# A diffusion layer on one core: gated tiles through another DMA queue, two early operand loads, and background steps placed later

## The chip, the cores and the metric

The kernel runs on one core of a Trainium2 chip. The core has five engines that each work through their own list of instructions in order: TensorE (PE, matrix products; PEld is its weight load), VectorE (DVE), ScalarE (ACT), GpSimd (POOL) and SyncE (SP, which here only issues DMAs). They wait for each other by semaphores. DMAs are carried by 16 shared DMA engines; an engine that issues one puts it in a queue, and here nearly all are issued by SP.

The metric is the device time of one execution in microseconds (us), lower being better.

## What is computed

One layer over 1024 latent tokens and 256 context tokens, 1024 channels wide, all in float32: a half-step SwiGLU feed-forward, then token mixing (a Fourier part and a bidirectional chunked mLSTM, merged by gates), then a second half-step feed-forward on the latent tokens.

```python
def swiglu(u, w13, w2):
    a, b = jnp.split(u @ w13, 2, axis=-1)
    return (jax.nn.silu(a) * b) @ w2

def half_ffn(h, shift, scale, gate, g_pre, g_post, w13, w2):
    u = modulate(rmsnorm(h, g_pre), shift, scale)
    return h + 0.5 * gate * rmsnorm(swiglu(u, w13, w2), g_post)

def ada_params(cvec, w, b):
    m = jax.nn.silu(cvec) @ w + b
    return m.reshape(cvec.shape[0], N_ADA, 1, D_MODEL)

def reference(...):
    ml = ada_params(c, w_ada[l], b_ada[l])
    mc = ada_params(c_ctx[None], w_ada[l], b_ada[l])
    h_lat = half_ffn(h_lat, ml[:, 0], ml[:, 1], ml[:, 2], g[0], g[1], w13_a[l], w2_a[l])
    h_ctx = half_ffn(h_ctx, mc[:, 0], mc[:, 1], mc[:, 2], g[0], g[1], w13_a[l], w2_a[l])
    h_lat, h_ctx_new = token_mixing(...)
    h_lat = half_ffn(h_lat, ml[:, 6], ml[:, 7], ml[:, 8], g[4], g[5], w13_b[l], w2_b[l])
    return h_lat
```

The hidden width of a feed-forward is 2816, the nine modulation vectors of each stream (shift, scale and gate for three sub-layers, called chunks 0 to 8 below) come from `ada_params`.

## The kernel before

**Products.** Every float32 operand is split by `split_act` into a rounded high part (ACT, L145) and the rest (DVE, L146); weights go the same way (L140/L141 in `wunit`, or `split_act`). A product of 128x128 by 128x512 is three matmuls, all at L153 in `mm3`. The large products of the two feed-forwards use a two-by-two scheme with seven products in place of eight, so DVE also adds and subtracts blocks of weights and of operands (L727 and others).

**The feed-forward.** `ffn_in` computes the first product pair by pair of column tiles, 11 pairs. Its operands for the second block of tokens are made in the background by `operands`, whose sums of two tiles run on GpSimd (L455, L456). Gated tiles ("m" and "t", 128x512) are the blocks that the seven products of the second matrix need; `gated` (L475) or the sums at L582/L583 finish a tile, and `put` (L478/L479) stores it to the DRAM scratch `gx`: four "m" tiles and three "t" tiles for each pair, 77 for each `ffn_in`, so 154 in all. L614 reads some of them back. `wino_out` is the second product: for n in (1, 6, 7, 4, 5, 3, 2) and each k it calls `operand` (L772 to L777), which loads a tile of `gx` into a "t" slot (L774) and splits it into two "g" slots, takes the weights (L733, L738), and issues 12 matmuls. The first `ffn_in` ends and the first `wino_out` begins at about 483 us of the trace, the second pair of stages meets at about 2510 us.

**Slots.** Tiles come from tags with a fixed number of slots ("t" 8, "m" 5, "g" 36, "ld" 2, "u" 16, "wa" 2, "b" and others); a new tile waits until the last user of its slot has finished.

**Background work.** Generators are advanced a step (a `yield`) at a time by `tick`. `later(gen, rate=r)` puts a generator in the list with a rate, and `tick(part)` adds part x rate to a credit that pays for steps. `wino_out` ticks 1/8 for each group of three matmuls, so at a rate of 3.5 one step falls on about 2.3 groups. Behind the first `wino_out` run `load_x` for the context (transposes at L375) and `ada_rest` for chunks 2 and 3, then the context's `prenorm` and `ada_rest` for chunk 4. `ada_rest` computes half a chunk for two streams: eight loads of weights (L247), 16 multiply-adds on DVE (L251, L253), one split for each stream (L145, L146), the sum over the partitions as matmuls on PE (L263), a copy of the row (L266), and transposes of the row back into columns (`ada_cols`, L275, added up at L279). There is one step between a split and its row sums, and one between the copy and the transposes. During the mLSTM heads `ada_rest` for one stream and chunks 5 to 8 runs as `self.side`, at a rate of 3.0. Behind the second `wino_out` runs `to_tokens` at a rate of 1.0, once for each block of 512 tokens: for each of eight channel tiles a load of `h` (L1556), a step, four transposes into a "qc" bank of PSUM (L1560), a copy (L1562) and a store to `h2t` (L1563).

**Order.** The code order is the order of calls above; the instructions of one engine are put in a final order by a scheduler when the program is built, and each engine then keeps that order. An instruction that waits holds up all that follow it on its engine. SP carries loads of weights, loads of `gx`, stores and background loads in one such list.

Of the kernel before, what the change touches and what calls it, by code (L numbers as in the profile page):

```python
# [15 lines left out]
P = 128  # L16
D = 1024
ND = D // P
SEQ = 1024
CTX = 256  # L20
# [14 lines left out]
class Kernel:  # L35
# [200 lines left out]
            nc.scalar.copy(row[:2, :], pt[:2, :])  # L236
            self.ada_cols(row, (0, 1), ch, 0)

    def ada_rest(self, streams, chunks, tags=("wa", "u", "u", "b"), halves=(0, 1)):
        nc = self.nc  # L240
        w = self.a["w_ada"][0]
        for ch in chunks:
            for hf in halves:
                acc = {s: self.s512(tags[1]) for s in streams}
                for k in range(ND):
                    t = self.s512(tags[0])
                    nc.sync.dma_start(t, w[k * P : (k + 1) * P, ch * D + hf * TB : ch * D + (hf + 1) * TB])  # L247
                    yield
                    for s in streams:
                        if k == 0:  # L250
                            nc.vector.tensor_scalar_mul(acc[s], t, self.sc[:, k, s : s + 1])  # L251
                        else:
                            nc.vector.scalar_tensor_tensor(acc[s], t, self.sc[:, k, s : s + 1], acc[s],  # L253
                                                           op0=ALU.mult, op1=ALU.add)
                yield
                for s in streams:
                    ah, al = self.s512(tags[2], F32R), self.s512(tags[2], F32R)
                    self.split_act(ah, al, acc[s])
                    if s == streams[0]:
                        pr = self.aux()  # L260
                    yield
                    for i, part in enumerate((ah, al)):
                        nc.tensor.matmul(pr[:2, :], self.sel[:, s, :], part, start=s == streams[0] and i == 0,  # L263
                                         stop=s == streams[-1] and i == 1)
                row = self.s512(tags[3])
                nc.scalar.copy(row[:2, :], pr[:2, :])  # L266
                yield
                self.ada_cols(row, streams, ch, hf)

    def ada_cols(self, row, streams, ch, hf):  # L270
# [205 lines left out]
        return gate  # L476

    def put(self, p, t, gx, n):  # L478
        self.nc.sync.dma_start(gx[n - 1, p * P : (p + 1) * P, :], t)  # L479

    def pair_weights(self, w, q, n0, W, p1s):

# [236 lines left out]
    def wino_out(self, w2, gx, tokens, done):  # L719
# [50 lines left out]
            return [(hi[:, c], lo[:, c]) for c in cs]  # L770

        def operand(n, k):  # L772
            t = self.s512("t")
            nc.sync.dma_start(t, gx[n - 1, k * P : (k + 1) * P, :])  # L774
            hi, lo = self.s512("g", F32R), self.s512("g", F32R)
            self.split_act(hi, lo, t)
# [774 lines left out]
    def to_tokens(self, scr, b, dst):  # L1551

        nc = self.nc
        for d in range(ND):
            t = self.s512("u")
            nc.sync.dma_start(t, scr[d * P : (d + 1) * P, b * TB : (b + 1) * TB])  # L1556
            yield
            pt = self.aux("qc")
            for j in range(4):
                nc.tensor.transpose(pt[:, j * P : (j + 1) * P], t[:, j * P : (j + 1) * P], self.ident)  # L1560
            o = self.s512("u")
            nc.scalar.copy(o, pt)  # L1562
            nc.sync.dma_start(dst[b * TB : (b + 1) * TB, d * P : (d + 1) * P].rearrange("(j p) c -> p j c", p=P),  # L1563
                                o.rearrange("p (j c) -> p j c", j=4))

    def final(self, h2t):
# [35 lines left out]
    def run(self):  # L1602
# [29 lines left out]
        for p in range(3):  # L1632
# [5 lines left out]
        gx = self.scratch([7, FF // 2, TB], "gx")  # L1638
        rc1, r1 = [], [[], []]
        self.ffn_in(w13, 11, u, U, gx, 6, mid)  # L1640
        self.later(self.load_x(a["ctx"][0], CTX, "c", xc, tag="u"), self.ada_rest([0, 1], [2, 3], "uuuu"),
                   rate=3.5)
        self.credit = -9.0
        uc = ctx_u([self.slot("u", F32R) for _ in range(ND)])

        def ctx_in():
            yield from self.prenorm(self.reload(xc[0], CTX), xc[1:], CTX, 1, 0, uc)
            yield from self.ada_rest([0, 1], [4])
        self.later(ctx_in(), rate=3.5)
        res = [[None] * ND for _ in range(NB)]  # L1650

# [52 lines left out]
        self.side_rate = 3.0  # L1704
        for h in range(HEADS):
            if h == 1:
                self.side = self.ada_rest([0], [5, 6, 7, 8], ("ld", "acc", "rb", "b"))
            if h % 2 == 0:
                v = [[self.slot("u") for _ in range(4)] for _ in range(2)]
                br = self.bias_row(C_V + h * DH)  # L1710
# [99 lines left out]
```

## Time and profile before

| | |
|---|---|
| median of 3 runs | 2758.67 us (2755.25 to 2763.62) |
| the profiled execution | 2761.97 us |
| its span in the trace | 2760.1 us |
| PE busy | 2661.3 us, 96% |
| DVE busy | 1857.2 us, 67% |
| ACT busy | 1106.8 us, 40% |
| POOL busy | 100.6 us, 4% |
| DMA traffic | 472.51 MB, mean 171 GB/s |
| mean granted PE clock | 0.986 |

The share of an engine is that of its busy time in the span. An average over the span hides that stages have different limits, so the prediction reads single stretches: views of the busy time in stretches of 60 us, the waits of an engine by the instruction that ended them, and timelines, where each row has a start in us, a duration, the engine and line, the tiles out<-in, the number of instructions in the row, and in brackets the idle time before it and what ended that. A granted clock under 1.00 means that PE ran its matmuls more slowly.

### The profile page before, as it was taken

What the parts mean: (1) busy time and instruction counts of PE and PEld (TensorE: products, weight loads), DVE (VectorE), ACT (ScalarE), POOL (GpSimd) and SP (SyncE); (2) the same over time, 40 slices, a digit from 0 to 9 for tenths busy, and PEclk for the clock granted to TensorE, in tenths of its full rate; (3) what the DMA queues carried; (4) which work ended last, traced back from release to release, by engine and by line L of the source; (5) the groups of instructions that cost most, each with busy time, mean ns of one, the idle gap of its engine ahead of it and who ended that gap; (6) DMA issues with size and microseconds to landing.
All of it is one profiled execution on the core that took longest, in us unless ns stands there. A gap on an engine that the chain in (4) does not pass through costs nothing.

```text
span 2760.1 us, 33923 instructions
## 1 busy us (share of the span) xinstructions
PE 2661.3 (96%) x11657; PEld 2114.7 (77%) x11657; DVE 1857.2 (67%) x3341; ACT 1106.8 (40%) x1893; POOL 100.6 (4%) x217
## 2 busy tenths in 40 slices
PE   8899999998999999999999999999999999998998
PEld 5688888776877777777777778778887788887776
DVE  5688887899786438565363674555667887863765
ACT  4543332444454337233333333433345433333552
POOL 1100000000000001000000000000001000000000
PEclk9999999999999999999999999999999999999999
DMA  9765454857686545325223452356556654536874
GB/s 300 242 206 164 155 167 133 309 190 252 210 252 211 170 134 173 102 69 155 79 77 103 133 142 77 94 150 196 181 157 210 183 169 153 168 107 198 293 247 139
DMA packets 426012, 472.51 MB, mean 171 GB/s; under 512 B 25497, under 2 KB 264642, under 8 KB 425840
## 3 DMA queue, kind: packets, MB, share of 16 engines
q1 hardware_dynamic: 424448, 468.53, 54.2%
q0 software_dynamic: 1248, 1.75, 0.2%
q8 instruction: 92, 1.51, 0.2%
q14 instruction: 80, 0.66, 0.1%
q10 hardware_dynamic: 144, 0.07, 0.0%
HBM read 373.21 MB, written 97.04 MB: 170 GB/s over the span
## 4 chain that ended last, share of the span: by engine, by line
PE 75%; DVE 9%; DMA 8%; issue 4%; ACT 2%; SPq 1%; POOL 0%; DVEq 0%; POOLq 0%; ACTq 0%
PE mm L153 67%; DMA m<-r_l 2%; PE aux L1147 2%; PE qc L1332 1%; DVE u L253 1%; DVE wl L141 1%; DVE g L146 1%; DMA ld<-in_w_ada_dram 1%; DMA ld<-h 1%; DMA u<-h 1%; DMA ld<-hn 1%; PE mm L234 1%; DMA t<-gx 0%; ACT wh L140 0%; DVE wl L146 0%
## 5 line engine op out<-in xcount | busy, mean ns | idle before, releaser
L153 PE MATMUL mm<-g,wh 128*128 128x512 f32 (+1 forms) x2552 | 839.6, 409 | 11.9 <-ACT g L145 5.0
L153 PEld LDWEIGHTS mm<-g,wh 128*128 128x128 f32 (+1 forms) x2552 | 484.2, 192 | 122.2 <-ACT wh L145 6.0
L153 PE MATMUL mm<-g,wl 128*128 128x512 f32 (+1 forms) x1276 | 510.7, 402 | 3.4 <-DVE wl L146 3.3
L153 PE MATMUL mm<-g,o 128*128 128x512 f32 x2112 | 497.7, 394 | 0.0
L153 PEld LDWEIGHTS mm<-g,o 128*128 128x128 f32 x2112 | 396.9, 188 | 93.7
L141 DVE TENSOR_TENSOR wl<-wr,wh 128x1024 fp32r<-128x1024 f32 x226 | 278.8, 1234 | 223.9 <-ACT wh L140 223.2
L140 ACT CAST wh<-wr 128x1024 fp32r<-128x1024 f32 x226 | 236.3, 1046 | 352.5 <-PE mm L153 307.3
L153 PE MATMUL mm<-wh,g 128*128 128x512 f32 x1032 | 331.2, 399 | 6.6 <-ACT g L145 3.9
L153 PEld LDWEIGHTS mm<-g,wl 128*128 128x128 f32 (+1 forms) x1276 | 243.8, 191 | 59.0 <-DVE wl L146 5.6
L153 PE MATMUL mm<-u,wh 128*128 128x512 f32 (+1 forms) x848 | 268.4, 398 | 7.5 <-DVE m L704 4.9
L153 PEld LDWEIGHTS mm<-wh,g 128*128 128x128 f32 x1032 | 194.1, 188 | 54.5 <-ACT g L145 4.1
L153 PE MATMUL mm<-wl,g 128*128 128x512 f32 x516 | 205.1, 397 | 0.0
L153 PEld LDWEIGHTS mm<-u,wh 128*128 128x128 f32 (+1 forms) x848 | 159.8, 190 | 46.0 <-DVE m L704 5.4
L153 PE MATMUL mm<-wh,u 128*128 128x512 f32 x544 | 176.4, 399 | 0.0
L153 PE MATMUL mm<-u,wl 128*128 128x512 f32 (+1 forms) x424 | 167.3, 397 | 2.3 <-DVE wl L141 2.3
L582 DVE TENSOR_TENSOR t<-mm,t 128x512 f32<-128x512 f32 x128 | 88.1, 688 | 78.8 <-PE mm L153 78.6
L146 DVE TENSOR_TENSOR g<-t,g 128x512 fp32r<-128x512 f32 x154 | 103.0, 687 | 38.9 <-ACT g L145 32.1
L153 PEld LDWEIGHTS mm<-wh,u 128*128 128x128 f32 x544 | 102.0, 188 | 22.5
L145 ACT CAST o<-wa 128x512 fp32r<-128x512 f32 x88 | 54.6, 622 | 156.0 <-PE mm L153 144.8
L145 ACT CAST wh<-wr 128x1024 fp32r<-128x1024 f32 (+1 forms) x72 | 62.5, 870 | 131.9 <-PE mm L153 55.2
L153 PEld LDWEIGHTS mm<-wl,g 128*128 128x128 f32 x516 | 97.2, 188 | 23.0 <-issue 0.7
L153 PE MATMUL mm<-wl,u 128*128 128x512 f32 x272 | 108.8, 400 | 2.1 <-DVE wl L141 2.1
(469 smaller groups left out, 3432.8 us busy)
## 6 DMA issues: line engine op xcount, KB each, us to landing
wr<-in_w_a_dram SPq DMA_DIRECT2D x124, 512.0 KB, 4.4
t<-gx SPq DMA_DIRECT2D x174, 256.0 KB, 4.0
wr<-in_w_in_dram SPq DMA_DIRECT2D x80, 512.0 KB, 3.8
wr<-in_w_b_dram SPq DMA_DIRECT2D x70, 512.0 KB, 4.5
gx<-m SPq DMA_DIRECT2D x88, 256.0 KB, 4.2
gx<-t SPq DMA_DIRECT2D x66, 256.0 KB, 4.3
ld<-in_w_ada_dram SPq DMA_DIRECT2D x64, 256.0 KB, 2.8
ld<-h SPq DMA_DIRECT2D x48, 256.0 KB, 3.8
```

What stands on the lines that cost most here:

```text
L140: nc.scalar.copy(hv, rv)
L141: nc.vector.tensor_tensor(lv, rv, hv.bitcast(F32), op=ALU.subtract)
L145: self.nc.scalar.copy(hi, src)
L146: self.nc.vector.tensor_tensor(lo, src, hi.bitcast(F32), op=ALU.subtract)
L153: mul = lambda x, y, start, stop: self.nc.tensor.matmul(out, x, y, start=start, stop=stop, skip_group_check=grown)
L234: nc.tensor.matmul(pt[:2, :], self.sc[:, k, :], t, start=k == 0, stop=k == ND - 1)
L253: nc.vector.scalar_tensor_tensor(acc[s], t, self.sc[:, k, s : s + 1], acc[s], op0=ALU.mult, op1=ALU.add)
L582: add = lambda o, x, y: nc.vector.tensor_tensor(o, x, y, op=ALU.add)
L1147: nc.tensor.matmul(pt[:, :257], kw[:, i * P : (i + 1) * P], vaug, start=True, stop=True)
L1332: nc.tensor.matmul(pt[:, :257], at(q, i, c), C[:, i * 257 : (i + 1) * 257], start=i == 0, stop=i == 1)
```

## The change

Four edits. `put` issues its store on GpSimd's queue in place of SP's. `operand` takes the first two tiles of n = 1 from "ld" in place of "t". `ada_rest` has a parameter `lag`, the number of further steps between a split and its row sums, and between the copy of the row and its transposes: 2 behind the first `wino_out`, 1 for the mLSTM side work, 0 elsewhere. `to_tokens` loads two channel tiles ahead of the transposes, and its stores go through GpSimd's queue. Line numbers of the changed kernel are 2 to 8 higher from there on (`put` L481, the row sums L264, the load of an operand L776, the transposes of `to_tokens` L1568).

```diff
-    def ada_rest(self, streams, chunks, tags=("wa", "u", "u", "b"), halves=(0, 1)):
+    def ada_rest(self, streams, chunks, tags=("wa", "u", "u", "b"), halves=(0, 1), lag=0):
...
                     self.split_act(ah, al, acc[s])
                     if s == streams[0]:
                         pr = self.aux()
-                    yield
+                    for _ in range(1 + lag):
+                        yield
                     for i, part in enumerate((ah, al)):
                         nc.tensor.matmul(pr[:2, :], self.sel[:, s, :], part, ...
                 row = self.s512(tags[3])
                 nc.scalar.copy(row[:2, :], pr[:2, :])
-                yield
+                for _ in range(1 + lag):
+                    yield
                 self.ada_cols(row, streams, ch, hf)
...
     def put(self, p, t, gx, n):
-        self.nc.sync.dma_start(gx[n - 1, p * P : (p + 1) * P, :], t)
+        self.nc.gpsimd.dma_start(gx[n - 1, p * P : (p + 1) * P, :], t)
...
         def operand(n, k):
-            t = self.s512("t")
+            t = self.s512("ld" if n == 1 and k < 2 else "t")
             nc.sync.dma_start(t, gx[n - 1, k * P : (k + 1) * P, :])
...
     def to_tokens(self, scr, b, dst):
         nc = self.nc
-        for d in range(ND):
-            t = self.s512("u")
-            nc.sync.dma_start(t, scr[d * P : (d + 1) * P, b * TB : (b + 1) * TB])
-            yield
+        ts = deque()
+        for d in range(ND + 2):
+            if d < ND:
+                t = self.s512("u")
+                nc.sync.dma_start(t, scr[d * P : (d + 1) * P, b * TB : (b + 1) * TB])
+                ts.append(t)
+            yield
+            if d < 2:
+                continue
+            t = ts.popleft()
             pt = self.aux("qc")
             for j in range(4):
                 nc.tensor.transpose(pt[:, j * P : (j + 1) * P], t[:, j * P : (j + 1) * P], self.ident)
             o = self.s512("u")
             nc.scalar.copy(o, pt)
-            nc.sync.dma_start(dst[..., d * P : (d + 1) * P]...
+            nc.gpsimd.dma_start(dst[..., (d - 2) * P : (d - 1) * P]...
...
-        self.later(self.load_x(...), self.ada_rest([0, 1], [2, 3], "uuuu"), rate=3.5)
+        self.later(self.load_x(...), self.ada_rest([0, 1], [2, 3], "uuuu", lag=2), rate=3.5)
...
-            yield from self.ada_rest([0, 1], [4])
+            yield from self.ada_rest([0, 1], [4], lag=2)
...
-                self.side = self.ada_rest([0], [5, 6, 7, 8], ("ld", "acc", "rb", "b"))
+                self.side = self.ada_rest([0], [5, 6, 7, 8], ("ld", "acc", "rb", "b"), lag=1)
```

The change moves instructions on each engine. Three places follow. First, SP's list where the first `ffn_in` meets the first `wino_out`, before; `t_4220` and `t_4226` are the first two operands of `wino_out`, `m_4082`, `m_4102` and `t_4195` the last gated tiles:

```order
L479 DMA gx<-m_4061 128x512
L479 DMA gx<-t_4172 128x512
L479 DMA gx<-t_4173 128x512
L479 DMA gx<-m_4082 128x512
L384 DMA xT_c<-u_4402 128x2x256
L479 DMA gx<-m_4102 128x512
L479 DMA gx<-t_4195 128x512
L774 DMA t_4220<-gx 128x512
L774 DMA t_4226<-gx 128x512
L774 DMA t_4266<-gx 128x512
```

SP's list at the same place in the changed kernel, where `t_4108` is the last tile that `ffn_in` itself reads back:

```order
L247 DMA wa_5851<-in_w_ada_dram 128x512
L247 DMA wa_5883<-in_w_ada_dram 128x512
L776 DMA ld_4226<-gx 128x512
L616 DMA t_4108<-gx 128x512
L740 DMA g_4212<-in_w_a_dram 128x512
L740 DMA g_4214<-in_w_a_dram 128x512
L740 DMA g_4258<-in_w_a_dram 128x512
L740 DMA g_4260<-in_w_a_dram 128x512
L776 DMA t_4266<-gx 128x512
L776 DMA t_4272<-gx 128x512
```

The stores have left SP's list, and the load of the second operand stands ahead of the load of `t_4108` (that of the first operand, `ld_4220`, stands five rows earlier). On PE the 16 short transposes of the context (L375), which stood between the last product of `ffn_in` and the first of `wino_out`, now stand behind 81 to 102 of its matmuls.

Second, PE's list at the first half chunk of `ada_rest` behind `wino_out`, before. `aux_4661` is the row of sums, `u_4657`/`u_4658` the parts of the first stream and `u_4670`/`u_4671` of the second; `mm_4206` to `mm_4209` are the four banks of `wino_out`:

```order
L263 MATMUL aux_4661<-u_4657,sel 2x512
L263 MATMUL aux_4661<-u_4658,sel 2x512
L153 MATMUL mm_4209<-g_4632,wh_4608 128x512
L153 MATMUL mm_4209<-g_4633,wh_4608 128x512
L153 MATMUL mm_4209<-g_4632,wl_4609 128x512
L153 MATMUL mm_4206<-g_4695,wh_4677 128x512
L153 MATMUL mm_4206<-g_4696,wh_4677 128x512
L153 MATMUL mm_4206<-g_4695,wl_4678 128x512
L263 MATMUL aux_4661<-u_4670,sel 2x512
L263 MATMUL aux_4661<-u_4671,sel 2x512
```

PE's list at the sums of the second stream (here `u_4710`/`u_4711`) in the changed kernel:

```order
L153 MATMUL mm_4207<-g_4747,wh_4729 128x512
L153 MATMUL mm_4207<-g_4748,wh_4729 128x512
L153 MATMUL mm_4207<-g_4747,wl_4730 128x512
L264 MATMUL aux_4661<-u_4710,sel 2x512
L264 MATMUL aux_4661<-u_4711,sel 2x512
L153 MATMUL mm_4208<-g_4747,wh_4729 128x512
```

Before, six matmuls of `wino_out` stood between the two streams' sums; now 30 stand between the sum of the first stream's first part and that of the second's. The first row sums of the six halves stand behind 177, 252, 340, 421, 560 and 649 matmuls of `wino_out` before, and behind 180, 292, 438, 552, 748 and 861 now.

Third, GpSimd's list in the first `ffn_in`, now, where `b_...` and `wa_...` are the sums of two tiles for `operands`:

```order
L457 TENSOR_TENSOR b_991<-u_198,u_206 128x512
L313 TENSOR_TENSOR rx_967<-rs_t_965,mhalf 128x4
L458 TENSOR_TENSOR wa_992<-u_202,u_210 128x512
L481 DMA gx<-m_960 128x512
L457 TENSOR_TENSOR b_1079<-u_199,u_207 128x512
L481 DMA gx<-m_1049 128x512
L458 TENSOR_TENSOR wa_1080<-u_203,u_211 128x512
L481 DMA gx<-m_1122 128x512
L458 TENSOR_TENSOR wa_1187<-u_204,u_212 128x512
L457 TENSOR_TENSOR b_1186<-u_200,u_208 128x512
```

Before, the same list has the sums and `rx_967` alone, without the stores between them. Over the whole program SP's list goes from 1514 rows to 1344, and GpSimd's from 199 to 369.

More of the change, by code (lines that the diff above doesn't have):

```diff
@@ L1562, in to_tokens @@
             nc.scalar.copy(o, pt)
-            nc.sync.dma_start(dst[b * TB : (b + 1) * TB, d * P : (d + 1) * P].rearrange("(j p) c -> p j c", p=P),
+            nc.gpsimd.dma_start(dst[b * TB : (b + 1) * TB, (d - 2) * P : (d - 1) * P].rearrange("(j p) c -> p j c", p=P),
                                 o.rearrange("p (j c) -> p j c", j=4))
@@ L1640, in run @@
         self.ffn_in(w13, 11, u, U, gx, 6, mid)
-        self.later(self.load_x(a["ctx"][0], CTX, "c", xc, tag="u"), self.ada_rest([0, 1], [2, 3], "uuuu"),
+        self.later(self.load_x(a["ctx"][0], CTX, "c", xc, tag="u"), self.ada_rest([0, 1], [2, 3], "uuuu", lag=2),
                    rate=3.5)
```

## The prediction

> **What bounds the kernel now.** I read the page first, then busy time in stretches of 60 us, then PE's waits, then timelines at the places these point to. In a row of the stretches stand: the stretch, its length, and busy us (with instructions) of PE, PEld, DVE, ACT and POOL, then the granted clock, the DMA share and GB/s.
>
> ```profile
> PE 2661.3 (96%) x11657; PEld 2114.7 (77%) x11657; DVE 1857.2 (67%) x3341; ACT 1106.8 (40%) x1893; POOL 100.6 (4%) x217
> 300.00:360.00 60.00, 60.00 (x261) 48.57 (x260) 46.95 (x74) 20.08 (x34) 0.00 (x0) 1.00 0.51 161
> 480.00:540.00 60.00, 55.04 (x237) 44.03 (x236) 47.85 (x79) 27.07 (x48) 0.00 (x0) 0.94 0.84 298
> 540.00:600.00 60.00, 54.48 (x224) 41.41 (x223) 55.91 (x94) 26.13 (x46) 0.00 (x0) 0.94 0.65 222
> 600.00:660.00 60.00, 53.86 (x227) 40.29 (x226) 56.00 (x92) 26.89 (x45) 0.00 (x0) 0.97 0.76 242
> 660.00:720.00 60.00, 56.84 (x238) 44.43 (x237) 54.32 (x84) 31.83 (x49) 1.39 (x1) 0.94 0.75 236
> 720.00:780.00 60.00, 59.77 (x275) 48.44 (x274) 44.40 (x60) 29.01 (x40) 2.94 (x2) 1.00 0.69 212
> 2520.00:2580.00 60.00, 55.22 (x259) 42.83 (x258) 35.44 (x56) 30.28 (x55) 0.00 (x0) 1.00 0.91 287
> ```
>
> PE is the bound, and an undisturbed stretch (300 to 360) holds 261 matmuls, 60/261 = 0.23 us each. What the change can win is only where PE falls short of that. 480 to 720 holds 926 in place of 1044: 118 fewer, 27 us. In three of those four stretches DVE is busy 54 to 56 of 60 us, so there PE is fed by DVE; at 720 DVE is at 44 and PE full again. The second place is 2520 to 2580, with DVE at 35.
>
> **The two starts of the second product.**
>
> ```profile
> PE mm L153 <- ACT g L145: 8.9, 2, 5.0
> 484.43 0.60 PE L375 MATMUL qc<-ident,u 128*128 128x128 f32 x4
> 490.00 1.52 PE L153 MATMUL mm<-g,wh 128*128 128x512 f32 x2 [4.96 <-ACT g L145]
> 495.58 0.95 PE L153 MATMUL mm<-g,wh 128*128 128x512 f32 x2
> 498.67 0.62 PE L153 MATMUL mm<-g,wh 128*128 128x512 f32 x2
> 486.12 0.32 SPq L479 DMA_DIRECT2D gx<-t  x1
> 486.49 2.38 SPq L774 DMA_DIRECT2D t<-gx  x5
> 489.32 0.62 ACT L145 CAST g<-t 128x512 fp32r<-128x512 f32 x1 [3.51 <-DMA t<-gx]
> ```
>
> The one large wait of PE for a split falls twice, once at each start. SP issues the last store at 486.12 and only then the first operand's load (486.49); it is split at 489.32, PE starts at 490.00 after 4.96 us idle. Then PE is slow: the pair at 495.58 still takes 0.95 us, that at 498.67 takes 0.62. By the timeline 12 matmuls stand between 490.00 and 495.58, 5.6 us for 12 x 0.23 = 2.8: another 2.8 us. The two loads now stand ahead of the last stores, into idle slots, and the order lets PE go straight on. The 16 transposes move behind it and cost the same there. Both 4.96 and 2.8 go: **7.8 us**.
>
> Here a rule bears on the row: the Trainium skill, page "TensorE: Matmul & The Clock Gate", section on HAM, has PE at half clock for a while after some 3.4 us of idleness. By it the 2.8 us are won only if the gap falls under that length; the trace agrees in the slow pair at 495.58, and the sum stays the same where the gap goes whole.
>
> ```profile
> 2516.52 0.50 PE L153 MATMUL mm<-wh,g 128*128 128x512 f32 x1 [3.89 <-ACT g L145]
> 2519.81 0.90 PE L153 MATMUL mm<-wh,g 128*128 128x512 f32 x2
> ```
>
> The second start is the same: 3.89 us idle, and to 2520.5 only seven matmuls and four short transposes (4.0 us for 1.6 + 0.4), about 2.0 us: **5.9 us**. What is late next: k = 2 is loaded to a "t" slot, 24 matmuls or 5.5 us after the start, and its SP row waits only for a slot that comes free early in both stages; k = 7 to 9 wait for the last stores, needed 19 us after the start. I take both gaps whole; bounds 0 to 13.7 for the two, since a load that waits for a store behind the queue would leave a part.
>
> **The row sums.**
>
> ```profile
> L253 DVE SCALAR_TENSOR_TENSOR u<-u,sc,u 128x512 f32<-128x512 f32 x56 | 37.9, 745 | 0.3 <-DMA u<-in_w_ada_dram 0.3
> L253 DVE SCALAR_TENSOR_TENSOR u<-wa,sc,u 128x512 f32<-128x512 f32 x28 | 19.5, 748 | 4.1 <-DMA wa<-in_w_ada_dram 4.1
> L251 DVE TENSOR_SCALAR u<-u,sc 128x512 f32<-128x512 f32 x8 | 3.5, 482 | 1.0 <-DMA u<-in_w_ada_dram 1.0
> L251 DVE TENSOR_SCALAR u<-wa,sc 128x512 f32<-128x512 f32 x4 | 1.8, 479 | 0.0
> L146 DVE TENSOR_TENSOR u<-u,u 128x512 fp32r<-128x512 f32 x12 | 8.2, 685 | 0.0
> 556.16 0.39 PE L263 MATMUL aux<-u,sel 128*2 128x512 f32 x1 [1.54 <-ACT u L145]
> 558.53 1.01 PE L263 MATMUL aux<-u,sel 128*2 128x512 f32 x2 [1.98 <-DVE u L146]
> PE aux L263 <- DVE u L146: 2.9, 3, 2.0
> ```
>
> First what the words of the edit promise: a row sum no longer waits for its split. PE's own waits at L263 are small (2.9, and 1.54 at 556.16), so by these rows alone it is 4.4 us, and the slow matmuls behind. But the moved order also spreads DVE's work, and that is larger. The five rows sum to 70.9 us for six halves: 11.8 us of DVE each. The rest of DVE in 480 to 720 is 214.1 - 70.9 = 143.2 us over 926 matmuls, 0.155 us each. The six row sums stand behind 177 to 649 matmuls before, one per 94; that is 21.6 us of PE, and 94 x 0.155 + 11.8 = 26.4 us of DVE: 4.8 us short, five times, 24 us. With 6 further steps in each half (18 for 12) they stand behind 180 to 861, one per 136: 31.3 us of PE against 32.9 of DVE, 1.6 short, 8 us. The difference is 16 us. A second count, DVE's whole list against PE's up to each matmul with the rows' durations, has the largest lead of DVE fall from 29 to 14, a gain of 15. The work put off (the residual of the second block, chunk 4) falls into the stages from 720 on, where DVE has 15 us to spare in 60. Stalls within DVE's list (a split waits for its load or for ACT) are not in these counts and remain, so I take **13**, bounds 0 and 24.
>
> **The transposes behind the second product.**
>
> ```profile
> PE qc L1560 <- DMA u<-h: 3.9, 7, 1.1
> PE qc L1560 <- ACT g L145: 1.1, 1, 1.1
> ```
>
> Eight gaps, 5.0 us, none long enough for a lower clock (1.00 in that stretch). Loads two steps ahead remove the wait for the load. Yet the DMA share is 0.91 there, and the 16 loads and 16 stores are pulled into an earlier, equally busy time. Bounds 0 to 5; I take **2.5**.
>
> **GpSimd's queue.** 154 stores and 16 of `to_tokens` leave SP, each 0.32 us there, and cost POOL an issue each.
>
> ```profile
> L1000 POOL DMA_DIRECT2D rb<-in_b_in_dram x4 | 2.3, 573 | 37.8 <-ACT u L408 29.6 <-PE aux L263 7.5 <-DVE o L1011 0.7
> DMA to landing us min/median/max: 3.5/4.0/4.3
> gx<-t SPq DMA_DIRECT2D x66, 256.0 KB, 4.3
> L455 POOL TENSOR_TENSOR b<-u,u x8: 1289/1770/3552, 94.6 to 2146.0; 128x512 f32<-128x512 f32 x8
> 94.11 0.33 SPq L479 DMA_DIRECT2D gx<-m  x1
> 94.57 1.80 POOL L455 TENSOR_TENSOR b<-u,u 128x512 f32<-128x512 f32 x1 [79.40 <-ACT b L367]
> 128.68 0.32 SPq L479 DMA_DIRECT2D gx<-m  x1
> 128.73 1.65 POOL L456 TENSOR_TENSOR wa<-u,u 128x512 f32<-128x512 f32 x1 [1.23 <-DVE m L475]
> ```
>
> 170 x 0.573 = 97 us of POOL, which was busy 100.6 of 2760: hidden. L1000's DMAs land 3.5 to 4.3 us after issue (row two), like SP's stores (4.3). The stage is at a DMA share of 0.51 (300 to 360). A store that waits for DVE now holds up what stands behind it on POOL, that is the sums L455/L456 in the first `ffn_in` (94 to 147 us), and their operands. But before, the stores were issued just ahead of them (94.11 and 94.57; 128.68 and 128.73): by these times only the issue, 0.57, comes on top, for at most 8 sums. SP no longer waits at stores, so loads behind them start earlier; the mLSTM side's row sums waited little. I take -1 for the sums and +0 for the rest; bounds -5 to +5.
>
> For the gain of the queue itself a rule speaks against it: the Trainium skill, "DMA: Bandwidth & Descriptors", section "Issuing engines are not separate DMA queues", has the 16 engines shared, so that another issuer saves only the sequencer's time. The trace's 0.32 us per issue is what that would save, off PE's path. By it the queue is worth nothing at the bandwidth, and the early loads would have done the starts alone.
>
> **Sum.** 7.8 + 5.9 + 13 + 2.5 - 1 = 28.2 us, from 2761.97 (the profiled execution) 2734. That execution lies 3.3 us above the median of the runs, 2758.67; against that it is 2731. I say 2732. Before, 0.3% of the time (8.3 us) is about what a measurement can tell from no change.
>
> **Rivals.**
>
> *Only the gaps go.* DVE remains the bound of the first `wino_out` until its work is done: spreading `ada_rest` merely moves the same 70.9 us, and the operands still wait for their splits. DVE's 54 to 56 of 60 us speak for it; the 15 us free per stretch behind 720 against. Then 13.7, less 1, and 0 to 3 for the rest: 2743 to 2746 against the median, and to 2750 if one gap leaves a part. Chance 0.18.
>
> *The gain is given back.* The loads start earlier where DMAs are already at 0.84 to 0.91, each load takes longer, and the first operands come no earlier than PE wants the third; or chunk 4's work meets the context's stage and is late there. For it: 0.91 in the second product; against: a share of 0.51 in `ffn_in` before the start, where the two loads now run. Part of the 13.7 and nothing else: about 2754. Chance 0.12.
>
> *Slower: software stores that land late.* GpSimd's work is stretched when DVE is busy: L455 takes 1289 to 3552 ns. If writing a store's descriptors is stretched in `ffn_in`, where DVE is busy 47 of 60 us, a gated tile's slot comes free late and DVE, then PE, waits. A pair of columns takes 168 matmuls, 38.6 us, and stores four "m" of five slots, so a slot is written again some 48 us on. If a tile is in use for half of that, an estimate, some 20 us remain for its store: from there this rival decides. At 22 us each pair would lose about 2 us, 22 pairs 44 us, net of 28 won: 2775. Against it: 573 ns and 4.0 us above. Chance 0.08. The Trainium skill, "GPSIMD Engine Reference", Key points, names this sharing of SBUF ports between GpSimd and VectorE; no run here shows it for a DMA's issue.
>
> **How the numbers follow.** The forecast's own case (all terms near what I took) spans 2716 to 2744, chance 0.62. Its lower end has 24 for 13 and 5 for 2.5: 2731 - 13.5 = 2717. The range reaches over the gaps' case and part of the third, to 2756, leaving out the slower case and the rest. Faster by over 0.3%: 0.62 + 0.18 = 0.80; within: 0.12; slower: 0.08.
>
> **What would show it.** In the trace of the changed kernel: no idle time between the last product of `ffn_in` and the first of `wino_out`, at 1.00 (7.8 and 5.9); in the next 240 us about 980 matmuls or more, with DVE still over 50 of 60 us (13); L1568 without waits for `u<-h` (2.5); L481 landing in 4 to 5 us, L457 not later than 95 us (the queue). Wrong would be: DVE's waits at 720 to 900 that were not there, a gap at L774's successor, or stores over 10 us to landing.

## The result, and the profile after

The changed kernel took **2720.35 us** (median of 4 runs, 2716.96 to 2731.05) against 2758.18 us before (4 runs); the ratio is 0.9865, with a 95% interval of 0.9841 to 0.9890. That is some 38 us less. The forecast was 2732 in a range of 2716 to 2756. The profiled execution after took 2721.47 us, with a span of 2719.7 us.

The page's first line and the 60-us stretches of the changed kernel, with the same columns as before (stretch, length, busy us of PE, PEld, DVE, ACT, POOL, then clock, DMA share, GB/s):

```profile
PE 2643.7 (97%) x11657; PEld 2109.1 (78%) x11657; DVE 1858.5 (68%) x3341; ACT 1104.7 (41%) x1893; POOL 194.9 (7%) x387
...
480.00:540.00 60.00, 58.03 (x262) 46.74 (x261) 48.10 (x78) 24.99 (x44) 3.24 (x6) 1.00 0.85 292
540.00:600.00 60.00, 55.70 (x236) 43.30 (x235) 56.55 (x95) 30.06 (x53) 0.00 (x0) 0.97 0.64 204
600.00:660.00 60.00, 58.14 (x257) 45.82 (x256) 55.86 (x90) 33.80 (x56) 0.00 (x0) 1.00 0.89 297
660.00:720.00 60.00, 57.98 (x257) 45.97 (x257) 48.12 (x73) 21.14 (x31) 0.00 (x0) 1.00 0.57 181
...
2484.00:2550.00 66.00, 65.94 (x312) 53.69 (x311) 49.15 (x79) 37.66 (x70) 10.89 (x16) 1.00 0.95 342
```

From 480 to 720 there are now 1012 matmuls where there were 926. The second start has moved from 2516 to 2485 us of the trace, so the stretch to set beside 2520 to 2580 of before is 2484 to 2550: PE is full there, at a DMA share of 0.95.

The two starts, on PE of the changed kernel (start, duration, line, tiles, count): no row has a bracket, so PE goes from the last product of `ffn_in` (`st`) straight to the first of `wino_out` (`g`), and at 2484 through the transposes.

```profile
483.79 0.62 PE L153 MATMUL mm<-st,wh 128*128 128x512 f32 x2
484.25 0.40 PE L153 MATMUL mm<-st,wl 128*128 128x512 f32 x1
484.48 0.63 PE L153 MATMUL mm<-g,wh 128*128 128x512 f32 x2
...
2484.08 1.04 PE L1568 MATMUL qc<-ident,u 128*128 128x128 f32 x8
2484.87 0.48 PE L153 MATMUL mm<-wh,g 128*128 128x512 f32 x1
```

To see where the time went I matched the two traces product by product: L153 runs 10056 times in both kernels, in nearly the same order, so the time from the one with number a to that with number b can be compared. Numbers count from 0 in order of time. The table gives, for stretches between two numbers, how much longer (+) or shorter (-) they took than in the profile of before, in us. It covers all kernels that were run, one profile each.

| stretch of products | 0 to 480 | 1836 to 1956 | 1956 to 2772 | 2772 to 3480 | 3480 to 4200 | 4200 to 6240 | 6240 to 9120 | 9120 to 9156 | 9156 to 9420 |
|---|---|---|---|---|---|---|---|---|---|
| what it is | begin | first start | rest of first second product | context stage | to the heads | mLSTM heads | to second `ffn_in`'s end | second start | transposes |
| us of before's trace | 31 to 166 | 480 to 518 | 518 to 744 | 744 to 922 | 922 to 1123 | 1123 to 1821 | 1821 to 2508 | 2508 to 2525 | 2525 to 2599 |
| changed kernel | 1.5 | -8.2 | -15.6 | 5.7 | 1.2 | -15.6 | 3.3 | -4.5 | -8.5 |
| the same, again | 1.0 | -8.2 | -16.4 | 4.8 | 1.3 | -14.8 | 7.8 | -4.5 | -8.5 |
| side lag 0 | -2.9 | -8.2 | -15.1 | 5.1 | -0.1 | -6.8 | 4.7 | -4.5 | -8.5 |
| side lag alone | -3.2 | -1.4 | -1.4 | -0.3 | -0.1 | -17.0 | 3.8 | 0.1 | 1.7 |
| lag 0 behind first second product | -1.4 | -8.2 | -0.7 | -2.2 | 0.0 | -15.0 | 3.4 | -4.5 | -8.5 |
| put on SP | -0.7 | -8.0 | -18.3 | 7.4 | 1.9 | -17.1 | 4.2 | -3.7 | -7.7 |
| operands in t | -1.7 | -0.5 | -21.5 | 8.4 | 1.2 | -9.8 | 7.3 | -2.7 | -8.5 |
| to_tokens as before | 1.7 | -8.2 | -18.5 | 5.9 | 1.3 | -12.0 | 5.3 | -5.1 | 4.6 |
| early operands alone | -3.0 | -7.9 | 2.8 | -1.1 | -0.1 | -5.3 | 1.7 | -5.4 | 4.4 |
| put alone | -0.6 | 0.5 | -0.3 | -0.2 | 0.0 | -3.8 | 3.5 | -2.1 | 2.5 |
| steps ahead of the half | -0.5 | -8.2 | -23.1 | 5.0 | 1.3 | -14.6 | 5.0 | -4.5 | -8.5 |
| stores of to_tokens on SP | -0.7 | -8.2 | -15.5 | 4.9 | 0.2 | -13.7 | 4.2 | -3.4 | -6.0 |
| rate 3.0 | -0.4 | -9.1 | -22.4 | 0.7 | 20.7 | -16.5 | 2.9 | -4.5 | -8.5 |

Two profiles of the changed kernel (rows one and two) agree to within 1 us but for one stretch (3.3 and 7.8). The profile of before is itself off by a few us: three kernels that leave the heads as they were (side lag 0, early operands alone, put alone) are 3.8 to 6.8 shorter there, and all are 1.7 to 7.8 longer from 6240 to 9120. So a figure under 8 us in those two stretches says nothing, and the heads' gain is about 10, not 15.6. Rows of kernels that are alike in a stretch differ by up to 5 us at the beginning, up to 3.5 in the rest of the first second product, and less than 2 at the two starts and the transposes.

A stretch between two products also holds the other matmuls that fall into it, so its figure changes when background work moves from one stretch to the next. Where this matters it is said below.

### The profile page after: what moved, and what is told of

It is laid out like the page before. It is cut to its first block, busy times and chain, and to the rows that moved or that the text cites. A ratio compares the mean times of both kernels' runs of the same rounds, so it can differ in the third digit from the quotient of the medians.

```text
span 2719.7 us, 34141 instructions
## 1 busy us (share of the span) xinstructions
PE 2643.7 (97%) x11657; PEld 2109.1 (78%) x11657; DVE 1858.5 (68%) x3341; ACT 1104.7 (41%) x1893; POOL 194.9 (7%) x387
## 4 chain that ended last, share of the span: by engine, by line
PE 75%; DVE 9%; DMA 8%; issue 5%; ACT 2%; SPq 1%; POOL 0%; DVEq 0%; POOLq 0%; ACTq 0%
PE mm L153 68%; DMA m<-r_l 2%; PE aux L1149 2%; DMA wr<-in_w_a_dram 2%; PE qc L1334 1%; DVE wl L141 1%; DVE u L253 1%; DMA ld<-in_w_ada_dram 1%; DMA ld<-xT 1%; DVE g L146 1%; DMA u<-in_w_ada_dram 1%; PE mm L234 1%; DMA ld<-h 0%; ACT wh L140 0%; DVE wl L146 0%
## 5 line engine op out<-in xcount | busy, mean ns | idle before, releaser
L153 PE MATMUL mm<-g,wh 128*128 128x512 f32 (+1 forms) x2552 | 827.8, 404 | 4.9 <-ACT wh L145 2.8
L153 PEld LDWEIGHTS mm<-g,wh 128*128 128x128 f32 (+1 forms) x2552 | 477.4, 189 | 108.1 <-ACT wh L145 3.7
L153 PE MATMUL mm<-g,wl 128*128 128x512 f32 (+1 forms) x1276 | 505.7, 398 | 1.6 <-DVE wl L146 1.6
L153 PE MATMUL mm<-g,o 128*128 128x512 f32 x2112 | 497.6, 395 | 0.0
L153 PEld LDWEIGHTS mm<-g,o 128*128 128x128 f32 x2112 | 397.6, 188 | 93.0
L153 PE MATMUL mm<-wh,g 128*128 128x512 f32 x1032 | 332.6, 399 | 2.7 <-DVE rs_t L311 1.4
L153 PEld LDWEIGHTS mm<-g,wl 128*128 128x128 f32 (+1 forms) x1276 | 240.7, 189 | 55.5 <-DVE wl L146 3.5
L153 PE MATMUL mm<-u,wh 128*128 128x512 f32 (+1 forms) x848 | 269.5, 400 | 5.2 <-DVE m L706 3.5
L153 PEld LDWEIGHTS mm<-wh,g 128*128 128x128 f32 x1032 | 194.5, 188 | 49.7 <-DVE rs_t L311 1.8
L153 PE MATMUL mm<-wl,g 128*128 128x512 f32 x516 | 204.4, 396 | 0.0
L153 PEld LDWEIGHTS mm<-u,wh 128*128 128x128 f32 (+1 forms) x848 | 160.2, 191 | 44.2 <-DVE m L706 3.9
L153 PE MATMUL mm<-wh,u 128*128 128x512 f32 x544 | 179.5, 404 | 2.0 <-ACT wh L140 2.0
L153 PE MATMUL mm<-u,wl 128*128 128x512 f32 (+1 forms) x424 | 167.4, 398 | 2.8 <-DVE wl L141 2.7
L153 PEld LDWEIGHTS mm<-wh,u 128*128 128x128 f32 x544 | 103.2, 190 | 24.8 <-ACT wh L140 2.4
L153 PEld LDWEIGHTS mm<-wl,g 128*128 128x128 f32 x516 | 97.3, 189 | 22.9 <-issue 0.7
L145 ACT CAST g<-t 128x512 fp32r<-128x512 f32 x150 | 88.5, 619 | 60.8 <-PE mm L153 39.3
```

Of the source, the lines that this page charges most:

```text
L145: self.nc.scalar.copy(hi, src)
L153: mul = lambda x, y, start, stop: self.nc.tensor.matmul(out, x, y, start=start, stop=stop, skip_group_check=grown)
```

## The experiments

Where the records below name times between 1134 and 1831 us for the heads, these count from 10.6 us ahead of the span; in the views it is 1123 to 1821.

### 1. The lag of the mLSTM side work, taken out

```diff
-self.side = self.ada_rest([0], [5, 6, 7, 8], ("ld", "acc", "rb", "b"), lag=1)
+self.side = self.ada_rest([0], [5, 6, 7, 8], ("ld", "acc", "rb", "b"))
```

> The changed kernel without the lag of the mLSTM side work (its ada_rest for chunks 5 to 8 has one step between split and row sums again, as before). Matched product by product, the changed kernel gained 15.5 us against before between 1134 and 1831 us of before's trace, in the mLSTM heads, where I had put nothing. Theory 1 (the lag of the side work): without it that gain goes, the median rises by 10 to 16 us to about 2733. Theory 2 (it comes from something else, the freed SP queue or the place at which the background steps fall): the stage keeps 12 us or more of its gain and the median stays within 5 us of 2720.

2732.10 us (4 runs), ratio to before 0.9909 (0.9892 to 0.9925). Theory 1 holds: 12 us of the changed kernel's gain go, and the heads stand at -6.8 in place of about -15.

### 2. The same lag alone

```diff
-self.side = self.ada_rest([0], [5, 6, 7, 8], ("ld", "acc", "rb", "b"))
+self.side = self.ada_rest([0], [5, 6, 7, 8], ("ld", "acc", "rb", "b"), lag=1)
```

> The kernel before with one thing alone: lag=1 for the mLSTM side work. Theory 1: 10 to 16 us faster than before, all of it between 1134 and 1831 us. Theory 2: within 5 us of before.

2747.19 us, ratio 0.9959 (0.9944 to 0.9974), 12 us faster than before (2759.05 in the same set): the edit gives alone what it costs to take out. Where it acts is in PE's waits in the heads, not at the row sums. The longest group there, for the time of the heads, in before, side lag 0, the changed kernel and side lag alone, in that order (us in total, times, longest):

```profile
PE aux L1147 <- DVE m L1326: 13.8, 6, 4.7
```

```profile
PE aux L1149 <- DVE m L1328: 13.6, 6, 4.8
```

```profile
PE aux L1149 <- DVE m L1328: 9.1, 6, 3.4
```

```profile
PE aux L1149 <- DVE m L1328: 8.8, 6, 2.3
```

L1147 (L1149 in the changed kernel) is a matmul of the heads that waits for DVE. PE's wait there falls by 4.5 to 5 us and the longest from 4.7 to 2.3 or 3.4. The rest is in PE's busy time, with a higher clock. Nearly all of the difference lies in the last third of the heads, between products 5600 and 6240, which is another stretch of time in each trace. In before, side lag 0, the changed kernel and side lag alone, in that order:

```profile
1580.50:1820.60 240.10, 227.28 (x1038) 181.43 (x1037) 144.56 (x414) 91.55 (x199) 9.44 (x23) 0.98 0.38 109
```

```profile
1555.30:1795.10 239.80, 227.42 (x1039) 181.45 (x1038) 144.75 (x414) 91.71 (x199) 9.47 (x23) 0.98 0.37 110
```

```profile
1559.20:1789.40 230.20, 221.83 (x1022) 178.26 (x1021) 144.38 (x411) 88.59 (x193) 10.13 (x23) 0.99 0.39 113
```

```profile
1570.20:1798.10 227.90, 220.30 (x1023) 176.82 (x1022) 144.57 (x411) 88.95 (x193) 10.16 (x23) 1.00 0.41 115
```

With the lag the same products take 10 to 12 us less. PE is idle for some 8 us in place of 12 to 13 and busy for 5 to 7 us less, at a mean granted clock of 0.99 and 1.00 in place of 0.98 and with some 16 other matmuls fewer among the products. DVE is busy for 144 to 145 us in all four: it does as much, in another distribution. The side work now reaches further (the last row sum starts at 1808 us, behind product 6240, before at 1743).

### 3. Lag 0 behind the first second product

```diff
-self.ada_rest([0, 1], [2, 3], "uuuu", lag=2)
+self.ada_rest([0, 1], [2, 3], "uuuu")
...
-yield from self.ada_rest([0, 1], [4], lag=2)
+yield from self.ada_rest([0, 1], [4])
```

> The changed kernel with lag 0 behind the first second product (chunks 2, 3 and 4); the side work keeps lag 1. My account (DVE's work for the row sums spread over more matmuls): the 15.4 us that were won between product 1920 and 2520 go, while the 7 us given back between products 2520 and 3480 come back, so 6 to 9 us slower than the changed kernel, about 2728; the start at 483 us keeps its gain. Rival (the row sums' own waits alone): 3 to 5 us slower, and DVE as busy between 540 and 720 us as in the changed kernel. Second rival (the early operands brought all of it): no change.

2727.80 us, ratio 0.9889 (0.9874 to 0.9904). The kernel of the next experiment, whose time is that of the changed one, ran in the same set at 2720.62: 7.2 us, the size expected. In the table the stretch of the first second product goes from -15.6 to -0.7, the context stage from +5.7 to -2.2 and the stretch behind it from 1.2 to 0, in all some 6 us. The stretches show PE starved again with DVE full:

```profile
540.00:600.00 60.00, 55.02 (x225) 41.43 (x226) 57.59 (x96) 28.70 (x51) 0.00 (x0) 0.94 0.58 189
600.00:660.00 60.00, 52.62 (x217) 38.97 (x216) 54.45 (x87) 25.91 (x44) 0.00 (x0) 0.97 0.81 260
```

### 4. The stores back on SP

```diff
-self.nc.gpsimd.dma_start(gx[n - 1, p * P : (p + 1) * P, :], t)
+self.nc.sync.dma_start(gx[n - 1, p * P : (p + 1) * P, :], t)
```

> The changed kernel with put on SP's queue again. If the queue itself is worth nothing and the early loads of the first two operands do the starts alone, both starts keep their gains of about 10 us and the median stays at 2720 within 4 us. If the stores have to leave SP for the loads to run ahead of them, a gap of 4 to 5 us comes back at each start, with slow matmuls behind it, and the median rises by 8 to 14 us to about 2731.

2720.62 us, ratio 0.9861 (0.9846 to 0.9876): the time of the changed kernel. Both starts keep their gain (-8.0 and -3.7). The queue of `put` is worth nothing in the time once the two operands have slots of their own (at the second start 0.8 us of the table).

### 5. The first operands in "t" slots again

```diff
-t = self.s512("ld" if n == 1 and k < 2 else "t")
+t = self.s512("t")
```

> The changed kernel with the first two operands of n = 1 in t slots again; stores on GpSimd's queue, lags and to_tokens as changed. If the two idle slots are what makes the starts (the stores' queue being worth nothing, as the run with put on SP showed), both gaps of 4 to 5 us and the slow matmuls come back: 12 to 15 us slower than the changed kernel, about 2733. If leaving SP's list is enough for the loads to come early, no more than 4 us slower.

2731.14 us, ratio 0.9890 (0.9868 to 0.9912), 10.8 us slower than the changed kernel in the same set (2720.34). PE's wait at the first start is back (us in total, times, longest):

```profile
PE mm L153 <- ACT g L145: 6.5, 2, 5.2
```

At the second start a wait of only 1.3 us came back, 1.8 us by the table (-2.7 in place of -4.5): there the gap is small without the early slots too. Experiment 12 shows that the queue of `put` alone does that. And where the first start loses 7.7 us, the rest of that second product wins 5.9, as it would if DVE sets the end there and a later start leaves it less to catch up; experiment 7 has the reverse (-7.9, then +2.8). So by the table the edit is worth some 6 us, by the medians 11; the difference lies in the heads and the stretch behind them, which the edit does not touch and one profile cannot settle.

### 6. `to_tokens` as before

```diff
-        for d in range(ND + 2):
-            if d < ND:
-                t = self.s512("u")
-                nc.sync.dma_start(t, scr[d * P : (d + 1) * P, b * TB : (b + 1) * TB])
-                ts.append(t)
-            yield
-            if d < 2:
-                continue
-            t = ts.popleft()
+        for d in range(ND):
+            t = self.s512("u")
+            nc.sync.dma_start(t, scr[d * P : (d + 1) * P, b * TB : (b + 1) * TB])
+            yield
...
-            nc.gpsimd.dma_start(dst[...
+            nc.sync.dma_start(dst[...
```

> The changed kernel with to_tokens as before (a load, a step, the transposes; stores on SP). My term of 2.5 us (bounds 0 to 5): 2 to 5 us slower than the changed kernel, with waits of the transposes for u<-h of some 4 us again and the second start kept. If the DMA share of 0.9 had kept the gain down: within 1 us.

2734.48 us, ratio 0.9899 (0.9876 to 0.9922): **14 us** slower than the changed kernel. At the second start the early operands still bring 5.1 us, but 4.6 more than before are lost behind it. PE's waits and SP's waits there (2480 to 2580, and to 2570 for SP), with the transposes at L1562 and the stores at L1565:

```profile
PE qc L1562 <- DMA u<-h: 7.8, 6, 2.8
```

```profile
SPq L1565 <- ACT u L1564: 46.2, 15, 11.3
```

SP's list stands for 46 us (31 before) at stores that wait for ACT's copy of a transposed tile, and the loads of `gx` and `h` behind them are late. In the changed kernel PE waits for nothing in that stretch, and SP's longest group there is one that waits for free slots, ahead of need:

```profile
SPq L776 <- DVE g L146: 28.6, 24, 4.8
```

### 7. The early operands alone

```diff
-t = self.s512("t")
+t = self.s512("ld" if n == 1 and k < 2 else "t")
```

> The kernel before with one thing alone: the first two operands of n = 1 in ld slots. If that edit alone makes both starts: the gaps of 4.96 and 3.89 us before L153 are gone, 10 to 14 us faster than before, unless DVE behind the first start (54 to 56 of 60 us) takes its part back; then 5 to 8 us faster, with only the second start kept. If the stores must leave SP's list too: within 4 us of before.

2753.36 us (10 runs), ratio 0.9962 (0.9949 to 0.9975), against 2761.11: 8 us faster. Both gaps are closed (-7.9 and -5.4), but 2.8 us come back in the DVE-bound rest of the first second product and 4.4 at the transposes. The second start alone is worth 1 us, not the 5 to 8 that I had expected with a first start taken back; what is left is mostly the first.

### 8. The changed kernel again

> The changed kernel once more, on the same chip as the three others, for comparison with them and to see how far two profiles of one kernel differ stage by stage: median 2720 within 5 us; each stretch of products within 2 us of the first profile where PE waits for nothing, and the mLSTM heads, where PE waits for short chains on DVE and ACT, within 4 us.

2720.34 us, ratio 0.9854 (0.9835 to 0.9872). Its profile is row two of the table: stretches agree to 1 us, the heads too, but one from 6240 to 9120 differs by 4.5, outside what I expected.

### 9. The same steps, ahead of each half

```diff
             for hf in halves:
+                for _ in range(lag * (len(streams) + 1)):
+                    yield
...
-                    for _ in range(1 + lag):
-                        yield
+                    yield
...
-                for _ in range(1 + lag):
-                    yield
+                yield
```

> The changed kernel with the same number of background steps in each half of ada_rest, but placed elsewhere: the six (side work: two) further steps stand ahead of the half's first load, and the row sums and transposes come one step after their split and copy, as before. It tells two theories of the lag apart, in both stages. Theory A (spreading: DVE's work comes in smaller portions of each stretch of matmuls, and the slack between split and sums does not matter): the gains stay, -15 us within 4 between products 1920 and 2520, -15 within 3 in the mLSTM heads, median 2720 within 4. Theory B (slack: PE no longer meets a split that is late): both gains go, the first stage falls back to +2 (as with lag 0), the heads to -6, median about 2738.

**2713.77 us** (2711.35 to 2715.79), ratio 0.9831 (0.9813 to 0.9849): spreading holds, and slack between a split and its row sums falls. The first row sums of the six halves stand 134 matmuls apart here, 136 in the changed kernel, 94 before. With one step between them, as before, the heads keep their gain (-14.6) and the first second product wins more (-23.1 in place of -15.6). The fastest of all kernels here, it is 6.6 us under the changed one, which ran in another set. In the stretches of this kernel DVE is as full as ever, and PE nearly so too:

```profile
540.00:600.00 60.00, 60.00 (x268) 47.92 (x268) 58.80 (x97) 33.12 (x58) 0.00 (x0) 1.00 0.67 218
600.00:660.00 60.00, 58.19 (x252) 45.23 (x251) 54.71 (x87) 29.66 (x48) 0.00 (x0) 1.00 0.90 301
```

PE's wait at the row sums in this stage is 0.7 us in two instances, while in the changed kernel, with two steps more for the split, it is 3.6, and with lag 0 (experiment 3) 3.6 as well. First this kernel, then the changed one:

```profile
PE aux L265 <- DVE u L146: 0.7, 2, 0.6
```

```profile
PE aux L264 <- ACT u L145: 3.6, 2, 2.0
```

Why the slack itself costs some 7 us was not tried: a tile of the split keeps its "u" slot longer then, and the steps fall elsewhere; neither was taken alone.

### 10. The stores of `to_tokens` on SP

```diff
-nc.gpsimd.dma_start(dst[...
+nc.sync.dma_start(dst[...
```

> The changed kernel with the stores of to_tokens on SP's queue; its loads still run two steps ahead. Undoing the whole edit cost 14 us. If the loads ahead make that: median within 4 us of 2720 and no waits of the transposes for u<-h. If the stores, which wait on SP for a copy and hold up the loads of gx behind them, are the cost: 6 to 14 us slower than the changed kernel, with waits for t<-gx or u<-h at the second start.

2724.79 us, ratio 0.9880 (0.9854 to 0.9906), 4.4 us slower than the changed kernel's 2720.34 in another set, which the intervals of the two alone do not tell apart; by the table, where the changed kernel's figures repeat to 0.1 us, 3.6 us of the 13.0 at the second start and its transposes go. So most of the edit is the loads two tiles ahead, and a part the queue: SP again waits at these stores (L1571), and one operand comes 2.2 us late.

```profile
SPq L1571 <- ACT u L1570: 34.1, 10, 11.7
```

```profile
PE mm L153 <- ACT g L145: 2.2, 1, 2.2
```

### 11. A lower rate behind the first second product

```diff
-self.later(..., self.ada_rest([0, 1], [2, 3], "uuuu", lag=2), rate=3.5)
+self.later(..., self.ada_rest([0, 1], [2, 3], "uuuu", lag=2), rate=3.0)
...
-self.later(ctx_in(), rate=3.5)
+self.later(ctx_in(), rate=3.0)
```

> The changed kernel with a rate of 3.0 in place of 3.5 for the background work behind the first second product, so that it is spread by a further sixth. If spreading still has something to win there (PE is short of about 10 us between 540 and 780 us): 2 to 5 us faster than the changed kernel. If the work put off meets the context's stage, where 7 us came back already: no change within 3 us, with more of it between products 2520 and 3480.

2731.39 us, ratio 0.9893 (0.9870 to 0.9916), 11 us slower than the changed kernel. The first second product wins 6.8 us more (-22.4), and the context stage loses less, but then 20.7 us are lost before the heads. In the stretches there PE falls to 51.7 and 55.7 us of 60 and the clock to 0.94:

```profile
900.00:960.00 60.00, 56.45 (x235) 42.92 (x234) 32.05 (x51) 22.73 (x37) 1.12 (x7) 0.94 0.53 164
960.00:1020.00 60.00, 55.65 (x232) 40.72 (x231) 20.89 (x34) 16.85 (x27) 2.97 (x4) 1.00 0.40 122
1020.00:1080.00 60.00, 51.67 (x231) 38.74 (x229) 50.40 (x115) 42.88 (x67) 8.28 (x40) 0.94 0.53 154
```

What was put off is then due at a point where the code runs all background work to its end. My second guess had the place wrong: not the context stage, but behind it. That the forced end is what costs the 20.7 was argued from the code and not tried.

### 12. The stores on GpSimd's queue alone

```diff
-self.nc.sync.dma_start(gx[n - 1, p * P : (p + 1) * P, :], t)
+self.nc.gpsimd.dma_start(gx[n - 1, p * P : (p + 1) * P, :], t)
```

> The kernel before with one thing alone: put on GpSimd's queue. My account (-1 us for the sums on GpSimd, nothing else) and the run with put back on SP say 2760 within 4 us; the stores are out of SP's list, so if the order on SP alone made the gaps at the starts, 6 to 10 us faster.

2760.82 us (10 runs), ratio 1.0005 (0.9996 to 1.0014). Nothing in the time, and the gap at the first start is as long as before:

```profile
489.90 1.52 PE L153 MATMUL mm<-g,wh 128*128 128x512 f32 x2 [5.46 <-ACT g L145]
```

At the second start it is not: there the gap falls from 3.89 to 1.25 us with this edit alone.

```profile
2513.01 0.50 PE L153 MATMUL mm<-wh,g 128*128 128x512 f32 x1 [1.25 <-ACT g L145]
```

By the table that start wins 2.1 us, and the transposes behind it lose 2.5.

## Why the prediction was right, and where it was not

The sign and the range were right; the point was 12 us too high. That the range held was in part luck: two terms were 12 us each too small (the heads and the transposes) and the row sums 6 too large, and the result lies 4 us above a lower end that had been reached with 24 us for the row sums and 5 for the transposes. Taken one by one:

**The starts (7.8 and 5.9): right as sizes.** The first brought 8.2 us in the table, the second 4.5 to 5.4 (4.5 in the changed kernel, with 12 transposes more in that stretch). That the slots suffice, without the queue, is shown by put on SP (both kept). At the first start the queue does nothing without them (put alone, +0.5; operands in t, -0.5); at the second it does about half of it (put alone -2.1, operands in t -2.7), which the prediction did not count. What the sum missed is that they do not add to what stands behind: at the first, 5.9 us move into the DVE-bound stretch or out of it (experiment 5), and at the second, with `to_tokens` as it was, 4.6 of 5.1 come back at the transposes (experiment 6). The rival in which the gain is given back was true of that place, without the fourth edit.

**The row sums (13): too high.** Experiment 9 shows that it is the spreading and not the slack, as the prediction had put it against the words of the edit. The stretch itself won 15.6, and both counts of DVE's list had said as much (15 and 16), but that agreement is partly chance. The residual of the second block has matmuls of its own: 16 at L347 (L349 now) and eight at L318. Before they stood in this stretch, now they stand in the context stage. First the stretch of before, then the context stage of the changed kernel:

```profile
L347 PE MATMUL aux<-ones,acc x16: 164/250/250, 693.7 to 728.1; 128*128 128x1 f32 x16
```

```profile
L349 PE MATMUL aux<-ones,acc x32: 163/250/251, 734.1 to 857.7; 128*128 128x1 f32 x32
```

The context stage in before and in the changed kernel:

```profile
744.00:921.80 177.80, 175.78 (x794) 141.23 (x793) 125.57 (x148) 93.28 (x115) 4.99 (x5) 1.00 0.71 221
```

```profile
721.60:904.90 183.30, 179.84 (x817) 144.97 (x816) 141.22 (x175) 99.26 (x127) 6.12 (x7) 0.99 0.75 235
```

PE is busy there for 4 us more and idle for 1.5 more. So the term that was too large is the one that puts the work put off at nothing, because it "falls into the stages from 720 on, where DVE has 15 us to spare in 60": DVE did take 16 us more in that stage, but PE, which is full, has to do its share of this work wherever it stands. 5.7 and 1.2 us were lost there. Net 6 us by the table, 7 by the medians.

**The transposes (2.5, bounds 0 to 5): mis-sized.** With all else in place the edit is worth 14 us by the medians and 12.5 by the table, 5.1 - 4.6 against 4.5 + 8.5. I took the bound from the gaps at L1560 in the trace of before, as if these were all that its late loads cost. They depend on when the second start comes: by the table that stretch loses 4.4 and 4.6 us where the operands come early and `to_tokens` is as before, 1.7 at most where the start is late. The wait for `u<-h` alone does not show it: 7.8 us with the early start, but 3.9 and 6.5 in two kernels that are alike there (before and side lag alone), so that the trace of before was also a low sample. SP's 31 us of waits at L1563 stood in the view of waits and were not counted as what they are: a bar in front of every load behind them. With the loads two tiles ahead that bar is worth 3.6 us (experiment 10); the rest is the loads.

**The heads (0): missed.** That the side work's row sums "waited little" was true, 0.6 us, and beside the point. I had counted spreading for the first second product and not where the same parameter spreads the same kind of work: by 2 steps in 11, over a stage where PE waits for short chains on DVE. It gives 12 us alone, and experiment 9 keeps the gain with the steps in another place.

**GpSimd's queue (-1): nothing, 0 us.** The forecast of it held: an issue of `put` takes 0.54 us and its stores land in 3.9 us (0.75 and 5.4 us for the 16 of `to_tokens`, 7.8 at most), and the sums are not late, the first at 95.09 us for 94.57. The three rows are of the changed kernel: the stores' group, their landing, the first sum.

```profile
L481 POOL DMA_DIRECT2D gx<-m x88: 539/539/617, 77.7 to 2484.1; - x88
...
DMA to landing us min/median/max: 2.2/3.9/7.2
```

```profile
95.09 1.27 POOL L457 TENSOR_TENSOR b<-u,u 128x512 f32<-128x512 f32 x1 [1.74 <-ACT b L369]
```

So the rival of late software stores is out: 7.2 us at most for `put`, far from 20 (half of the 48 us would be 24). The rule of the Trainium skill, page "DMA: Bandwidth & Descriptors", section "Issuing engines are not separate DMA queues", by which another issuer saves only the sequencer's time, agrees with 1.0005 for put alone. In experiment 10 3.6 us do hang on the queue, but not by its speed: a store that waits for ACT no longer stands ahead of loads in the same list.

**In all.** 7.8 + 5.9 + 13 + 2.5 - 1 was 28; undone one by one, the edits are worth 11 (operands, by the table 6), 7 (lag), 14 (`to_tokens`), 12 (side lag) and 0 (put), which is 44 for the 38 that all of them bring together. Parts that need each other would give such an excess, but four differences of medians with a few us of uncertainty each can give 6 us as well.

## What to carry to other kernels

Before an edit that gives a waiting instruction more time is credited with that wait, count what it does to the portions of work per stretch on the engine that is full: here the steps worked by spreading DVE's work, and worked better where they gave no slack at all. An in-order list of DMAs is read by what stands behind each entry that waits: a store that waits for a copy costs the loads behind it, and the gaps of one trace need not show that cost. Work that is put off takes its share of the full engine with it: look at what it runs there too, not only at the spare time of the engine that was short. And how far it can be put off is limited by the next point at which all of it must be done, which is the likely reason for the 11 us that a lower rate lost.

## What was not expected of the hardware

GpSimd's issue of a store of `put` takes 539 ns in the median and 617 at most over the 154 of them, in stages in which DVE is busy 45 to 51 of 60 us, while its sums in the same stages vary from 1267 to 3529 ns. The same stores take fewer and larger packets. Put alone (experiment 12) takes 22176 packets from the hardware queue (424448 to 402272) and adds 12320 to the software queue (1248 to 13568), 144 against 80 for each of its 154 stores; the 16 stores of `to_tokens` take 528 against 80 each. The bytes are the same, and so nearly is the share of the DMA engines' time (all 170: 3.9% of the span less, 4.3% more). Before, put alone, and the changed kernel:

```profile
q1 hardware_dynamic: 424448, 468.53, 54.2%
q0 software_dynamic: 1248, 1.75, 0.2%
```

```profile
q1 hardware_dynamic: 402272, 428.15, 50.4%
q0 software_dynamic: 13568, 42.13, 4.0%
```

```profile
q1 hardware_dynamic: 393824, 423.96, 50.3%
q0 software_dynamic: 14848, 46.33, 4.5%
```
